# A hybrid decoder layer on one core: the first supertile of x by tokens only, turned on TensorE and scaled from PSUM; order of the adaLN staging tiles and the planner's DMA rate

## The chip, the core and the metric

One core of a Trainium2 chip runs the whole program. The engines are TensorE (PE; its weight loads are shown apart as PEld), VectorE (DVE), ScalarE (ACT), GpSimd (POOL) and SyncE (SP), which issues nearly all DMAs. The metric is the device time of one execution in microseconds (us).

## What is computed

One decoder layer on x of 4096 tokens by 1024 channels, float32. Cut to what matters here:

```python
shift, scale, gate = jnp.split(silu(c) @ ada_w + ada_b, 3, axis=-1)          # adaLN
h    = _rmsnorm(x, g_pre) * (1.0 + scale) + shift
proj = h @ w_in
attn = _sliding_window_attention(aq, ak, av, sinks) * silu(ag)
rwkv = _rwkv7_mixer(h, rr, rk, rv, ...) * silu(rg)      # recurrence over the tokens
gla  = _gla_mixer(h, gq, gkk, gv, ...) * silu(gg)
y    = jnp.concatenate([attn, rwkv, gla], axis=-1) @ w_out
return x + gate * _rmsnorm(y, g_post)
```

## The kernel before

The tokens are cut into 16 supertiles of 256. A first stage (to line 1567) makes h of each supertile, runs the GLA and RWKV-7 mixers over them in order, and stores h and the mixers' output to DRAM. A second stage does attention, the gates and the output product. The change touches the start of the first stage and, by the planner, the order of all engines.

**Precision.** A float32 matrix product is made of half-precision parts. Every weight is scaled by a power of two that comes from its sum of squares (`pow2`, line 434) and split: `hi` is a ScalarE instruction with that scale, `lo` the rest, by VectorE (`split_w`, line 731). h is split likewise into `hT[:, 0]` and `hT[:, 1]`; its power, `hscale`, comes from the adaLN vectors, and its inverse goes into the scale of each weight (`finish_w`, line 751). Each product is three: hi by hi, hi by lo, lo by hi.

**Start of the first stage.** SP loads the constants, the weights of GLA's values (`gv`), of its gate (`gk1`) and of the RWKV low-rank parts (`L`), the first 128 tokens of x (`xh`, for the sums of squares), x of supertile 0 by channels (`xt`, 1 MB, from the copy `xc` that the host has laid out), and then adaLN's matrix, 16 pieces of 128x1024 float32 (512 KB each). TensorE multiplies each piece as it lands (`adp`). Eight pieces lie in tiles of their own (`aw`); the other eight, like the weights, take staging tiles by turns from tiles that are used for something else later: the list `RING` (line 675) gives the turn, `half_tile` (line 679) takes the next. A tile that is taken twice makes the second load wait for the first one's readers. RA and UV have two tiles, KB one, and AT two that are cut in halves.

When the last piece is in, the sums are copied (`adrow`), turned (`adt`) and made into `sh` (shift) and `gs` (scale times norm weight); two ScalarE squares (`junk`), a TensorE sum (`hp`) and VectorE steps make `hscale` and `hinv`; `gs` and `sh` are multiplied by `hscale`.

**Stage a** (`stage_a`, line 1014) makes h of a supertile: squares of the tokens by rows (`ssx`), the inverse root on GpSimd (`rsx`), which TensorE turns and spreads over the partitions (`rb`), two VectorE products `xt * rb`, then for each of eight channel blocks a ScalarE instruction `xt*gs + sh`, and for each pair of blocks `hT` hi on ScalarE and lo on VectorE. The first half of supertile 0's tokens and its channels are loaded at the start, the second half of its tokens after adaLN's pieces.

**Stage p** (`stage_p`, line 1050) projects hT: `pv` (GLA values), `lp` (low rank; `x1` is read from it by VectorE), `zz` three times (k, r, v of RWKV) and `gqk` (GLA queries and keys). The weights k, r, v and gqk of the first supertile are loaded after adaLN and split in `stage_l` (line 831). `stage_d` and `stage_qa` make decays and keys (`rn`, `RA`, `KB`, with `ep` and `em`), `stage_k` turns KB (`kp`), `stage_q2` is the recurrence (`rp`, `up`, `sp`, `yp`, `yt`). The projections take turns in two PSUM tiles (`pj`).

**The planner.** Every instruction of a stage is recorded (`note`, line 99) with a modelled duration, and `pin` (line 222) plays a list schedule over all of them and fixes the order on each engine. `stage_l` has a lag of 150 places in rank (line 35). A DMA's bytes go through one modelled pipe (line 278). An engine then runs its instructions strictly in that order. As one helper emits all of them, they have the line 336 in the profile.

Of the kernel before, what the change touches and what calls it, by code (L numbers as in the profile page):

```python
# [12 lines left out]
F32 = mybir.dt.float32  # L13
# [50 lines left out]
class Order:  # L64
# [157 lines left out]
    def pin(self):  # L222

        steps = self.steps
        ready = {e: {} for e in ENGINES}
        bursts, head = {}, list(range(len(steps)))
        for k, st in enumerate(steps):
            if st.eng == "PE":
                h = head[k - 1] if k else 0
                if k and steps[h].eng == "PE" and st.joint and st.joint == steps[h].joint and st.array[0] == steps[h].array[0]:  # L230
                    head[k] = h
                bursts.setdefault(head[k], []).append(k)
        left, when = [0] * len(steps), [0.0] * len(steps)
        for k, st in enumerate(steps):
            for j in [*st.needs, *st.turn]:
                if head[j] != head[k]:
                    left[head[k]] += 1
                    steps[j].then.append(k)
        for k, st in enumerate(steps):
            if head[k] == k and not left[k]:  # L240
                ready[st.eng][k] = 0.0
        free = dict.fromkeys(ENGINES, 0.0)
        cells, mode, table, pipe, half = [0.0] * 16, None, None, 0.0, {}
        last, count = {}, 0
        while count < len(steps):
            e = min((e for e in ENGINES if ready[e]), key=lambda e: max(free[e], min(ready[e].values())))
            now = max(free[e], min(ready[e].values())) + 1e-9
            at = sorted((k for k, t in ready[e].items() if t <= now), key=lambda k: (steps[k].rank, k))
            k = at[0]
            if e == "PE" and mode is not None and steps[k].array[0] != mode:  # L250

                same = [q for q in at if steps[q].array[0] == mode]
                wait = max(now - ready[e][q] for q in at if steps[q].array[0] != mode)
                if same and (mode != (4, 4) or wait < TILING_WAIT):
                    k = same[0]
            first = max(free[e], ready[e].pop(k))
            for k in bursts.get(k, [k]):
                st, t = steps[k], max(first, free[e])
                if e == "PE":
                    m, at, passes, took, issue = st.array  # L260
                    if mode is not None and m != mode:
                        t = max(t, max(cells)) + 0.094
                    mode = m
                    t = max(t, max(cells[c] for c in at))
                    for c in at:
                        cells[c] = t + passes * took
                    free[e], st.end = t + issue * passes, t + passes * took + 0.165
                else:
                    if st.half is not None:
                        was, half[e] = half.get(e, st.half), st.half  # L270
                        if was[0] != st.half[0] or None not in (was[1], st.half[1]) and was[1] != st.half[1]:
                            t = max(t, free[e] + 0.115)
                    if st.table is not None and st.table != table:
                        t, table = max(t, free[e] + 1.28), st.table
                    free[e], st.end = t + st.occ, t + st.lat
                    if st.bytes:

                        pipe = max(pipe, t + 1.7) + st.bytes / 310e3
                        st.end = max(st.end, pipe)
                st.start = t  # L280
                if e in last:
                    self.tc.add_manual_dep(
                        st.ins, last[e], mybir.DependencyInfo(mybir.DependencyClass.NoSync, mybir.DependencyReason.DATA))
                last[e], count = st.ins.name, count + 1
                for q in st.then:
                    to, h = steps[q], head[q]
                    left[h] -= 1
                    at = t if k in to.turn else 0.0
                    if k in to.needs and e != to.eng:
                        at = max(at, st.end + HOP_FROM[e] + HOP_INTO.get(to.eng, 0.0))  # L290
                    elif k in to.needs and (e == "SP" or e != "PE" and to.needs[k]):
                        at = max(at, st.end + (0.05 if e == "SP" else 0.03))
                    when[h] = max(when[h], at)
                    if not left[h]:
                        ready[to.eng][h] = when[h]
        self.forget()
# [104 lines left out]
def hybrid_kernel(ctx, tc, x, xc, rows, ada1, adaw, w1, wl, w2, wo, cst, abias, out):  # L401
# [21 lines left out]
    def vcol(name, j=None):  # L423
        a, b = VC[name]
        return vt[:, a:b] if j is None else vt[:, a + j : a + j + 1]
# [73 lines left out]
    def t_x(name="xt"):  # L499
        return sp_.tile([P, 2, D], F32, tag="xt", name=name, bufs=1)  # L500
# [139 lines left out]
    with ExitStack() as p1:  # L640
# [14 lines left out]
        def wt(shape, name, bufs=1, dt=F32, tag=None):  # L655
            tag = tag or name
            return wk1[tag].tile(shape, dt, tag=tag, name=name, bufs=bufs)
# [14 lines left out]
            return wt(shape, name, 2, dt, "c3")  # L672


        RING = ("RA", "UV", "KB", "RA", "AT", "AT", "AT", "AT")
        stc = itertools.count()
        atq = []

        def half_tile(tag=None):
            tag = tag or RING[next(stc) % len(RING)]  # L680
            if tag == "AT":
                if not atq:
                    t = t_A([P, 2, 1024], "stg")
                    atq.extend(t[:, a, :] for a in range(2))
                t = atq.pop(0)
            else:
                t = wt([P, 1024], "stg" + tag, 2 if tag in ("RA", "UV") else 1, tag=tag)
            return t
# [14 lines left out]
        def load_tokens(i, a):  # L703
            xh = wt([P, D], "xh", 1)
            SP.dma_start(xh, x[i * NT + a * P : i * NT + (a + 1) * P, :])
            E[i]["xh"] = xh

        def load_channels(i):
            xt = E[i]["xt"] = t_x().rearrange("p a d -> p (a d)").rearrange("p (k t) -> p k t", k=KD)
            SP.dma_start(xt, xc[i])  # L710
# [11 lines left out]
        def w_pieces(n):  # L722

            r = []
            for h in range(2):
                t = half_tile()
                SP.dma_start(t, w1[:, n * 2048 + h * 1024 : n * 2048 + (h + 1) * 1024])
                r.append((slice(4 * h, 4 * h + 4), t.rearrange("p (k c) -> p k c", k=4)))
            return r
# [36 lines left out]
        mu_c = pp.tile([P, 6], F32, name="mu_c")  # L766
        V.tensor_scalar(mu_c, vcol("mu"), -1.0, 1.0, op0=ALU.mult, op1=ALU.add)

        gvp = w_pieces(0)
        gks = wt([P, KD, 16], "gk1s", 1, tag="gl")  # L770
        SP.dma_start(gks, w1src(5))
        wlt = half_tile().rearrange("p (k c) -> p k c", k=KD)
        SP.dma_start(wlt, wl)
        load_tokens(0, 0)
        load_channels(0)

        def early():
            yield from split_w("gv", gvp)
# [29 lines left out]
        def columns(j):  # L808
            return adt[:, :, j : j + 2, 0].rearrange("p c j -> p j c")

        V.tensor_tensor(sh.rearrange("p (j c) -> p j c", j=2), columns(0), vcol("bsh").rearrange("p (j c) -> p j c", j=2), op=ALU.add)
        V.tensor_tensor(gs.rearrange("p (j c) -> p j c", j=2), columns(2), vcol("bsc").rearrange("p (j c) -> p j c", j=2), op=ALU.add)
        V.scalar_tensor_tensor(gs, gs, 1.0, vcol("npre"), op0=ALU.add, op1=ALU.mult)
        hs = st.tile([P, 4], F32, tag="hs", name="hs")
        junk8 = st.tile([P, KD], F32, tag="junk8", name="junk8")
        S.activation(junk8, gs, AF.Square, scale=math.sqrt(2048.0), accum_out=hs[:, 0:1])
        S.activation(junk8, sh, AF.Square, scale=math.sqrt(2.0), accum_out=hs[:, 1:2])
        V.tensor_add(hs[:, 2:3], hs[:, 0:1], hs[:, 1:2])
        hp = mt("hp")
        PE.matmul(hp[:, 0:1], ones, hs[:, 2:3], start=True, stop=True)  # L820
        V.tensor_copy(hs[:, 3:4], hp[:, 0:1])
        pow2(hscale, hinv, hs[:, 3:4])
        V.tensor_scalar(gs, gs, hscale, None, op0=ALU.mult)
        V.tensor_scalar(sh, sh, hscale, None, op0=ALU.mult)

        for name in ("gv", "gk1", "L"):
            finish_w(name)
# [186 lines left out]
        def stage_a(i):  # L1014

            yield [("a", i - 1), ("p", i - 2)]
            e = E[i]
            ssx = st.tile([P, 2], F32, tag="ssx", name="ssx")
            for a in range(2):
                if i or a:  # L1020
                    load_tokens(i, a)
                yield [e["xh"]]
                S.activation(e["xh"], e["xh"], AF.Square, accum_out=ssx[:, a : a + 1])
            if i:
                load_channels(i)
            xt = e["xt"]
            yield [ssx]
            msx = st.tile([P, 2], F32, tag="msx", name="msx")
# [1206 lines left out]
```

## Time and profile before

| | us |
|---|---|
| three runs | 2020.94, 2021.44, 2027.34 |
| median | 2021.44 |
| the profiled execution | 2023.94 |
| its span | 2022.1 |
| granted TensorE clock over the span | 0.989 |

The profile shows one execution. Its page gives busy time by engine; the windows give the same for any stretch; the timeline lists instructions in order with start and duration, and for an idle time before an instruction what ended it. In names like `zz<-hT,rh`, the left is written and the right is read.

### The profile page before, as it was taken

The numbers are of one execution on the slowest core, as the hardware profiler recorded it, in microseconds if no ns is written. First come the engines' busy times: TensorE is split into PE (matmuls) and PEld (weight loads), VectorE is DVE, ScalarE is ACT, GpSimd is POOL, SyncE is SP. The second block draws the span as 40 slices with busy tenths as digits, with TensorE's granted clock in tenths as the row PEclk, the third lists the DMA queues.
The fourth block names the chain that finished last, engine by engine and source line by source line (L and its number), as shares of the span: only waits on it lengthen the run. The fifth ranks groups of instructions, "written<-read, shape, count | busy, mean of one in ns | idle before, by whom it ended". The sixth has DMA issues, their size and how long they took to land.

```text
span 2022.1 us, 59931 instructions
## 1 busy us (share of the span) xinstructions
PE 1919.5 (95%) x24899; PEld 1483.7 (73%) x24899; DVE 1506.7 (75%) x4246; ACT 1130.1 (56%) x2609; POOL 311.3 (15%) x485
## 2 busy tenths in 40 slices
PE   5899999999999999999989999999999999999997
PEld 1677787777787777877767678877778777787683
DVE  5777877887778887776758876777767777676866
ACT  5878778765866765555434544444454444444443
POOL 0622213262221222221100000000000000000001
PEclk8899999999999999999999999999999999999998
DMA  9464535353424411124243433344333443334414
GB/s 373 150 208 148 164 114 160 118 150 110 131 76 147 151 37 60 61 76 141 93 152 125 154 106 117 117 139 139 97 108 116 149 129 112 110 108 141 128 36 168
DMA packets 154267, 258.77 MB, mean 128 GB/s; under 512 B 49026, under 2 KB 100738, under 8 KB 147716
## 3 DMA queue, kind: packets, MB, share of 16 engines
q1 hardware_dynamic: 153844, 254.34, 38.8%
q8 instruction: 198, 3.24, 0.6%
q14 instruction: 81, 0.66, 0.1%
q10 hardware_dynamic: 144, 0.52, 0.1%
HBM read 193.98 MB, written 60.82 MB: 126 GB/s over the span
## 4 chain that ended last, share of the span: by engine, by line
PE 54%; DVE 22%; ACT 9%; DMA 8%; issue 4%; SPq 2%; POOL 1%; DVEq 0%; ACTq 0%; POOLq 0%
PE gp L336 16%; PE op L336 12%; PE zz L336 4%; PE qp L336 3%; PE pv L336 2%; PE lp L336 2%; PE kp L336 2%; PE sc L336 2%; DVE pr L336 2%; PE ovp L336 2%; DVE q L336 2%; DVE mtp L336 2%; SPq L336 2%; DMA cs<-in_wo 1%; DVE tsc L336 1%
## 5 line engine op out<-in xcount | busy, mean ns | idle before, releaser
L336 PEld LDWEIGHTS <-mtp 128*128 128x128 f16 x1344 | 130.7, 98 | 146.0 <-issue 6.3
L336 PE MATMUL op<-o,mtp 128*128 128x512 f16 x768 | 172.9, 380 | 0.0
L336 ACT ACTIVATE pr<-pr,nm,lsc 128x256 f32<-128x256 f32 (+1 forms) x256 | 149.0, 584 | 11.5 <-DVE nm L336 11.4
L336 PE MATMUL op<-ov,mtp 128*128 128x512 f16 x576 | 144.0, 381 | 3.6 <-DMA ov<-woscr 3.5
L336 PEld LDWEIGHTS <-hT 128*128 128x128 f16 x1536 | 120.5, 100 | 24.5 <-issue 3.9
L336 ACT ACTIVATE mtp<-yv,oi 128x1024 f16<-128x1024 f32 x30 | 34.5, 1149 | 155.1 <-DVE yv L336 114.4
L336 DVE CUSTOM_DVE_ANT_0 pr<-sc,ab,kept 128x256 f32<-128x256 f32 (+1 forms) x256 | 108.4, 475 | 15.5 <-PE sc L336 15.2
L336 POOL TENSOR_TENSOR ry<-sy,expo 128x1 f32<-128x1 f32 x30 | 19.1, 638 | 588.3 <-DVE sy L336 588.3
L336 PE MATMUL pv<-gvh,hT 128*128 128x272 f16 x512 | 101.0, 290 | 5.6 <-ACT hT L336 2.6
L336 DVE TENSOR_TENSOR yv<-op,yv 128x512 f32<-128x512 f32 x105 | 70.3, 681 | 47.3 <-PE op L336 33.4
L336 DVE SCALAR_TENSOR_TENSOR ag<-ag,gp 128x512 f32<-128x512 f32 x64 | 43.4, 678 | 67.8 <-ACT ag L336 67.7
L336 PE MATMUL zz<-hT,rh 128*128 128x256 f16 x512 | 91.8, 277 | 1.7 <-DVE x L336 1.7
L336 PE MATMUL lp<-hT,Lh 128*128 128x256 f16 x512 | 91.3, 274 | 1.7 <-issue 1.6
L336 PE MATMUL zz<-hT,kh 128*128 128x256 f16 x512 | 91.9, 273 | 0.0
L336 ACT ACTIVATE ag<-gp,gh 128x512 f32<-128x512 f32 x64 | 43.9, 686 | 83.3 <-PE gp L336 83.3
L336 PE MATMUL qp<-hT,q1h 128*128 128x256 f16 x512 | 86.3, 273 | 3.7 <-DVE kT L336 3.7
L336 PE MATMUL zz<-hT,vh 128*128 128x256 f16 x512 | 89.4, 275 | 0.0
L336 PE MATMUL gqk<-hT,gqkh 128*128 128x256 f16 x512 | 87.5, 273 | 1.1 <-DVE zb L336 1.1
L336 PE MATMUL gp<-hT,q5h 128*128 128x256 f16 x512 | 86.3, 273 | 0.0
L336 PE MATMUL qp<-hT,q0h 128*128 128x256 f16 x512 | 85.4, 273 | 0.0
L336 PE MATMUL gp<-hT,q3h 128*128 128x256 f16 x512 | 85.3, 273 | 0.0
L336 PE MATMUL gp<-hT,q6h 128*128 128x256 f16 x512 | 85.2, 273 | 0.0
(442 smaller groups left out, 5858.5 us busy)
## 6 DMA issues: line engine op xcount, KB each, us to landing
ov<-woscr SPq DMA_DIRECT2D x96, 512.0 KB, 4.5
xh<-in_x SPq DMA_DIRECT2D x32, 512.0 KB, 4.2
xt<-in_xc SPq DMA_DIRECT2D x16, 1024.0 KB, 8.3
hscr<-hT SPq DMA_DIRECT2D x16, 1024.0 KB, 5.0
hT<-hscr SPq DMA_DIRECT2D x16, 1024.0 KB, 4.8
x<-in_x SPq DMA_DIRECT2D x30, 512.0 KB, 4.3
out<-yv SPq DMA_DIRECT2D x30, 512.0 KB, 3.0
cs<-in_w SPq DMA_DIRECT2D x56, 256.0 KB, 3.5
```

The costliest lines, as they stand in the source:

```text
L336: r = f(*args, **kw)
```

## The change

x of supertile 0 is no longer loaded by channels. Both halves of its tokens (two loads of 512 KB into the tile of `xt`) are loaded first of all after the constants. ScalarE squares them, GpSimd makes the inverse root, VectorE scales the rows, and sixteen TensorE transposes put them by channels into four PSUM tiles, all ahead of adaLN. After adaLN, ScalarE scales from PSUM with `gs0` and `sh0`, which are not yet multiplied by `hscale`, into float32 (`hf`, in the same tile as the tokens); `hT` hi is made from that with `hscale` as its scale, and lo on VectorE with `hscale` as its column. `hscale` is thus needed one step later. `RING` now lists all turns of the start, with the AT halves ahead of RA. In `pin` a load's bytes pass at 400 instead of 310 GB/s; the same figure in the class that guides the recording (line 379) stays.

```diff
-                        pipe = max(pipe, t + 1.7) + st.bytes / 310e3
+                        pipe = max(pipe, t + 1.7) + st.bytes / 400e3
...
-        RING = ("RA", "UV", "KB", "RA", "AT", "AT", "AT", "AT")
+        RING = ("RA", "UV", "KB", *["AT"] * 4, "RA", "RA", "UV", "KB", *["AT"] * 4, "RA", "RA", "UV", "KB")
...
+        x0 = t_x()
+        for a in range(2):
+            SP.dma_start(x0[:, a], x[a * P : (a + 1) * P, :])
         gvp = w_pieces(0)
...
-        load_tokens(0, 0)
-        load_channels(0)
+
+        def first_x():
+
+            junk = wt([P, D], "xh", 1)
+            ssx = st.tile([P, 2], F32, tag="ssx", name="ssx")
+            for a in range(2):
+                S.activation(junk, x0[:, a], AF.Square, accum_out=ssx[:, a : a + 1])
+            msx = st.tile([P, 2], F32, tag="msx", name="msx")
+            V.tensor_scalar(msx, ssx, 1.0 / D, 1e-6, op0=ALU.mult, op1=ALU.add)
+            rsx = st.tile([P, 2], F32, tag="rsx", name="rsx")
+            rsqrt(rsx, msx, 2)
+            turned = []
+            for a in range(2):
+                V.tensor_scalar(x0[:, a], x0[:, a], rsx[:, a : a + 1], None, op0=ALU.mult)
+            for n, tag in enumerate(("tr", "y", "sq", "pj")):
+                tp = pst(tag, "tp").rearrange("p (a n) -> p a n", a=2)
+                for kk in range(2):
+                    k = 2 * n + kk
+                    for a in range(2):
+                        PE.transpose(tp[:, kk, a * P : (a + 1) * P], x0[:, a, k * P : (k + 1) * P], ident)
+                turned.append(tp)
+            return turned
+
+        turned = first_x()
...
+        gs0, sh0 = [cp.tile([P, KD], F32, name=n) for n in ("gs0", "sh0")]
...
-        V.tensor_scalar(gs, gs, hscale, None, op0=ALU.mult)
-        V.tensor_scalar(sh, sh, hscale, None, op0=ALU.mult)
+        V.tensor_scalar(gs, gs0, hscale, None, op0=ALU.mult)
+        V.tensor_scalar(sh, sh0, hscale, None, op0=ALU.mult)
...
+            if i == 0:
+                hT = e["hT"] = t_hT()
+                hf = x0.rearrange("p a d -> p (a d)").rearrange("p (k t) -> p k t", k=KD)
+                for kp, tp in enumerate(turned):
+                    ks = slice(2 * kp, 2 * kp + 2)
+                    for kk in range(2):
+                        k = 2 * kp + kk
+                        S.activation(hf[:, k], tp[:, kk], AF.Identity, scale=gs0[:, k : k + 1], bias=sh0[:, k : k + 1])
+                    S.activation(hT[:, 0, ks], hf[:, ks], AF.Identity, scale=hscale)
+                    V.scalar_tensor_tensor(hT[:, 1, ks], hf[:, ks], hscale, hT[:, 0, ks], op0=ALU.mult, op1=ALU.subtract)
+                    yield
+                SP.dma_start(hscr[i], hT.rearrange("p a k t -> p (a k t)"))
+                return
```

How the planned order moves, at three places. First ScalarE from the end of adaLN to the first hT; `kh` are squares of the k weights, `xh` squares of x. Before:

```order
L336 COPY adrow<-adp 128x512
L336 ACTIVATE junk_448,hs<-gs 128x8
L336 ACTIVATE junk_448,hs<-sh 128x8
L336 ACTIVATE xh,ssx<-xh 128x1024
L336 ACTIVATE kh,wss_537<-stgRA 128x1024
L336 ACTIVATE kh,wss_537<-stg 128x1024
L336 ACTIVATE xt<-xt,sh,gs 128x256 x3
L336 ACTIVATE hT<-xt 128x512
```

And of the change:

```order
L336 COPY adrow<-adp 128x512
L336 ACTIVATE junk_479,hs<-gs_473 128x8
L336 ACTIVATE junk_479,hs<-sh_474 128x8
L336 ACTIVATE xt<-tp,sh_474,gs_473 128x256 x5
L336 ACTIVATE hT<-xt,hscale 128x512 x2
L336 ACTIVATE xt<-tp,sh_474,gs_473 128x256 x2
L336 ACTIVATE hT<-xt,hscale 128x512
L336 ACTIVATE xt<-tp,sh_474,gs_473 128x256
```

The squares of x and k no longer stand between adaLN and the scaling of x. Second, VectorE where the low half of the gqk weights (`gqkl`) is made in the first supertile; `x` is `x1`, `k` and `zb` are keys and mixed projections. Before:

```order
L336 TENSOR_TENSOR xt<-xt,rb 128x1024
L336 SCALAR_TENSOR_TENSOR x_801<-lp,ivL,bl 128x256
L336 SCALAR_TENSOR_TENSOR gqkl<-stgUV,wsc,gqkh 128x1024
L336 SCALAR_TENSOR_TENSOR gqkl<-stgKB,wsc,gqkh 128x1024
L336 SCALAR_TENSOR_TENSOR gl<-gp,ga 128x256
```

And of the change, some forty rows behind `x`:

```order
L336 TENSOR_TENSOR k_1051<-k_1051,zb_800 128x512
L336 SCALAR_TENSOR_TENSOR ta<-ta,rn 128x512
L336 SCALAR_TENSOR_TENSOR sq_1143<-zb_862,first,k_1051 128x256
L336 SCALAR_TENSOR_TENSOR sq_1143<-zb_862,first,k_1051 64x256
L336 SCALAR_TENSOR_TENSOR gqkl<-stgUV,wsc,gqkh 128x1024
L336 TENSOR_TENSOR hT<-xt,hT 128x512
L336 SCALAR_TENSOR_TENSOR gqkl<-stgKB,wsc,gqkh 128x1024
```

The split of gqk has moved from beside x1 to behind the keys (`rn`, `RA`). Third, TensorE around the recurrence's first product `yp`. Before, behind the last of the gqk projection:

```order
L336 LDWEIGHTS gqkl
L336 MATMUL gqk<-hT,gqkl 128x256
L336 MATMUL yp<-Sst_502,RA 64x64 x4
L336 MATMUL kp<-first,KB 128x128 x4
L336 LDWEIGHTS hT
L336 MATMUL pv<-gvh,hT 128x272
```

And of the change, behind the last of v's projection:

```order
L336 LDWEIGHTS vl
L336 MATMUL zz<-hT,vl 128x256
L336 MATMUL yp<-Sst_533,RA 64x64 x4
L336 LDWEIGHTS gqkh
L336 MATMUL gqk<-hT,gqkh 128x256
```

The gqk projection has moved from ahead of `yp` to behind it. In the second stage the orders are the same but for a few rows.

More of the change, by code (lines that the diff above doesn't have):

```diff
@@ L679, in half_tile @@
         def half_tile(tag=None):
-            tag = tag or RING[next(stc) % len(RING)]
+            tag = tag or RING[next(stc)]
             if tag == "AT":
@@ L809, in columns @@
             return adt[:, :, j : j + 2, 0].rearrange("p c j -> p j c")
-        V.tensor_tensor(sh.rearrange("p (j c) -> p j c", j=2), columns(0), vcol("bsh").rearrange("p (j c) -> p j c", j=2), op=ALU.add)
-        V.tensor_tensor(gs.rearrange("p (j c) -> p j c", j=2), columns(2), vcol("bsc").rearrange("p (j c) -> p j c", j=2), op=ALU.add)
-        V.scalar_tensor_tensor(gs, gs, 1.0, vcol("npre"), op0=ALU.add, op1=ALU.mult)
+        gs0, sh0 = [cp.tile([P, KD], F32, name=n) for n in ("gs0", "sh0")]
+        V.tensor_tensor(sh0.rearrange("p (j c) -> p j c", j=2), columns(0), vcol("bsh").rearrange("p (j c) -> p j c", j=2), op=ALU.add)
+        V.tensor_tensor(gs0.rearrange("p (j c) -> p j c", j=2), columns(2), vcol("bsc").rearrange("p (j c) -> p j c", j=2), op=ALU.add)
+        V.scalar_tensor_tensor(gs0, gs0, 1.0, vcol("npre"), op0=ALU.add, op1=ALU.mult)
         hs = st.tile([P, 4], F32, tag="hs", name="hs")
         junk8 = st.tile([P, KD], F32, tag="junk8", name="junk8")
-        S.activation(junk8, gs, AF.Square, scale=math.sqrt(2048.0), accum_out=hs[:, 0:1])
-        S.activation(junk8, sh, AF.Square, scale=math.sqrt(2.0), accum_out=hs[:, 1:2])
+        S.activation(junk8, gs0, AF.Square, scale=math.sqrt(2048.0), accum_out=hs[:, 0:1])
+        S.activation(junk8, sh0, AF.Square, scale=math.sqrt(2.0), accum_out=hs[:, 1:2])
         V.tensor_add(hs[:, 2:3], hs[:, 0:1], hs[:, 1:2])
@@ L1017, in stage_a @@
             e = E[i]
+            if i == 0:
[11 more added lines that the diff above has]
+                return
             ssx = st.tile([P, 2], F32, tag="ssx", name="ssx")
             for a in range(2):
-                if i or a:
-                    load_tokens(i, a)
+                load_tokens(i, a)
                 yield [e["xh"]]
                 S.activation(e["xh"], e["xh"], AF.Square, accum_out=ssx[:, a : a + 1])
-            if i:
-                load_channels(i)
+            load_channels(i)
             xt = e["xt"]
```

## The prediction

> **What bounds the kernel now.** I read the page first, then the windows of stretches, then the timeline of the first 100 us on the engines that end waits there, and the waits of TensorE. The page, and one line of its chain of waits:
>
> ```profile
> span 2022.1 us, 59931 instructions
> PE 1919.5 (95%) x24899; PEld 1483.7 (73%) x24899; DVE 1506.7 (75%) x4246; ACT 1130.1 (56%) x2609; POOL 311.3 (15%) x485
> ...
> PE 54%; DVE 22%; ACT 9%; DMA 8%; issue 4%; SPq 2%; POOL 1%; DVEq 0%; ACTq 0%; POOLq 0%
> ```
>
> TensorE is the engine that sets the time. The same by stretches (span, then busy us and count by engine, granted clock, DMA share, GB/s):
>
> ```profile
> 0.00:34.50 34.50, 18.01 (x70) 3.58 (x70) 13.54 (x67) 11.97 (x20) 2.06 (x16) 1.00 0.96 372
> 34.50:43.60 9.10, 2.52 (x11) 1.71 (x11) 7.77 (x36) 6.57 (x16) 1.04 (x2) 0.65 1.03 410
> 43.60:103.00 59.40, 49.96 (x418) 38.98 (x418) 44.19 (x103) 52.13 (x100) 34.43 (x42) 0.85 0.54 173
> 103.00:1000.00 897.00, 861.67 (x14037) 694.61 (x14036) 704.53 (x2189) 606.95 (x1325) 238.09 (x372) 0.99 0.38 119
> 1000.00:2022.00 1022.00, 987.35 (x10366) 744.85 (x10366) 736.71 (x1855) 452.43 (x1152) 35.73 (x53) 0.99 0.38 122
> ```
>
> To 34.5 us DMA is the limit (0.96), to 43.6 a chain of small steps, to 103 ScalarE and VectorE feed the first supertile and TensorE is short of work by 9.4 us. From 103 it has work nearly always. So what the change wins must be won before 103 us, and be still there at 103.
>
> The steps it touches, from the timeline (start, duration, engine, line, instruction, idle before and its releaser):
>
> ```profile
> 23.19 0.33 SPq L336 DMA_DIRECT2D stgKB<-in_ada  x1
> ...
> 32.12 1.05 PE L336 MATMUL adp<-stgUV,scolb 128*32 128x512 f32 x4 [0.23 <-DMA stgUV<-in_ada]
> 33.40 1.05 PE L336 MATMUL adp<-stgKB,scolb 128*32 128x512 f32 x4 [0.23 <-DMA stgKB<-in_ada]
> 34.50 0.59 ACT L336 COPY adrow<-adp 128x512 f32<-128x512 f32 x1 [12.46 <-PE adp L336]
> 35.14 0.66 PE L336 MATMUL adt<-first,adrow 128*128 128x128 f32 x4 [0.69 <-ACT adrow L336]
> ...
> 36.95 0.18 ACT L336 ACTIVATION_READ_ACCUMULATOR junk<-sh 128x1 f32 x1
> 37.05 1.04 ACT L336 ACTIVATE xh<-xh 128x1024 f32<-128x1024 f32 x1
> ...
> 39.02 0.14 DVE L336 TENSOR_SCALAR hscale<-p2f 128x1 int32<-128x1 int32 x1
> ...
> 39.46 0.69 PE L336 MATMUL rb<-first,rsx 128*128 128x128 f32 x2 [1.49 <-POOL rsx L336]
> ...
> 41.44 1.58 ACT L336 ACTIVATE xt<-xt,sh,gs 128x256 f32<-128x256 f32 x3 [1.04 <-DVE xt L336]
> 42.93 0.61 ACT L336 ACTIVATE hT<-xt 128x512 f16<-128x512 f32 x1
> 43.60 0.41 PE L336 MATMUL pv<-gvh,hT 128*128 128x272 f16 x1 [2.55 <-ACT hT L336]
> ```
>
> **The loads.** Ahead of the last adaLN piece stood half of x by tokens (512 KB) and x by channels (1 MB); now 1 MB of tokens stands there. One 512 KB piece less, and pieces land 1.28 us apart (32.12 to 33.40): the last lands 1.28 us earlier. The other token half came after it, at no cost to it. Pieces lie in flight for 10.2 us (issue 23.19, use 33.40), about eight of them, so an issue that waits costs nothing until it is that late. In the new ring (AT tiles ahead of RA) the sixth adaLN piece that takes a ring tile waits until the first half of gv is split, with six pieces queued ahead of it and the rest of adaLN behind; the eight in flight are its cover, 10 us, beyond which each us late is a us late at the end.
>
> **Earlier work for x.** Two squares of 1.04 us (one from 37.05) move to the start; two VectorE scalings of 128x1024, with no row of this kind, cost between half and the whole of kl's 1.28 us (below) each; one power on GpSimd; sixteen transposes cost a quarter of adt's 0.66 each, 2.6 us in all. All lie in the stretch to 34.5 us, in which ScalarE was busy for 12.0 us, VectorE for 13.5 and TensorE for 18.0. The weights gv, gk1 and L come two pieces, 2.6 us, later, and are split in the same stretch; their users are pv and lp. If that cover were gone, 2.6 us would be paid.
>
> **adaLN to the first projection.** All of it is 1.28 us earlier: the junk squares end at 35.8 instead of 37.05. Then ScalarE went on to the square of x's second half, two squares of k, and an idle 1.04 us waiting for the multiplication by rb; now it scales from PSUM at once. One such instruction lies between half of hT's 0.61 (512 columns) and the SBUF form (1.58 for three, 0.53); I take 0.45, the time of zs below, a read from PSUM of this size. Five end at 38.0; hscale is there at 37.9; the first hT is done at 38.65, and pv starts at 38.7: **4.9 us earlier**, 4.5 or 5.6 by the two ends. The scaled hT is some 0.1 us longer (gqkh's 1.15 below against xh's 1.04), four times, which takes back what the reads from PSUM gain.
>
> **From there to 103 us.** The marks of before:
>
> ```profile
> 47.98 0.61 ACT L336 ACTIVATE hT<-xt 128x512 f16<-128x512 f32 x1
> 48.11 1.28 DVE L336 SCALAR_TENSOR_TENSOR kl<-stgRA,wsc,kh 128x1024 f16<-128x1024 f32 x1 [0.84 <-ACT kh L336]
> ...
> 52.29 0.38 PE L336 MATMUL lp<-hT,Lh 128*128 128x256 f16 x2
> ...
> 67.57 1.15 ACT L336 ACTIVATE gqkh<-stgUV,wsc 128x1024 f16<-128x1024 f32 x1
> ...
> 69.62 0.48 DVE L336 SCALAR_TENSOR_TENSOR x<-lp,ivL,bl 128x256 f32<-128x256 f32 x1
> 70.15 0.58 PE L336 MATMUL zz<-hT,rh 128*128 128x256 f16 x2 [1.71 <-DVE x L336]
> ...
> 71.39 1.47 DVE L336 SCALAR_TENSOR_TENSOR gqkl<-stgKB,wsc,gqkh 128x1024 f16<-128x1024 f32 x1
> 73.25 0.45 ACT L336 ACTIVATE zs<-zz,mu_s 128x256 f32<-128x256 f32 x1
> 74.37 0.42 PE L336 MATMUL zz<-hT,rl 128*128 128x256 f16 x1
> ...
> 86.09 0.38 PE L336 MATMUL gqk<-hT,gqkh 128*128 128x256 f16 x2
> ...
> 87.32 0.71 ACT L336 ACTIVATE rn<-rn,lnb 128x512 f32<-128x512 f32 x1
> 88.07 1.29 DVE L336 SCALAR_TENSOR_TENSOR rn<-zb,kkh,rn 128x256 f32<-128x256 f32 x1 [1.75 <-ACT rn L336]
> 89.88 0.47 DVE L336 SCALAR_TENSOR_TENSOR rn<-zb,kkh,rn 128x256 f32<-128x256 f32 x1
> 91.22 0.27 PE L336 MATMUL gqk<-hT,gqkl 128*128 128x256 f16 x1
> ...
> 96.22 0.39 PE L336 MATMUL pv<-gvh,hT 128*128 128x272 f16 x1 [1.40 <-DVE zb L336]
> ...
> 103.04 1.10 PE L336 MATMUL atp<-RA,KB 64*64 64x128 f32 x32
> ```
>
> ScalarE is the feeder, so I walk through its new order with these durations. The last hT is ready at 43.0 (was 48.6). TensorE needs some 7.5 us for pv, half of it at half clock, and starts lp at 46.4 (was 52.3). k's power waits behind pv on TensorE: wsc at 47.7, k split to 49.9, r's squares to 52.2, x's square and small ones to 54.5, r's wsc at 55.1, r split to 57.3, v's squares to 59.6, zs to 60.3. VectorE ends rl at 58.8, then the two multiplications of supertile 1 by 61.1, zb by 61.9, v's power, zlT, an hT half and mu by 64.5, then x1. So the r projection, which waits for x1, starts at 64.9 (was 70.15): 5.2 us ahead. From x1 to rn's second table took 17.7 us (69.62 to 87.32); the new row of work is 1 to 2 us shorter, because gqk's split (two of 1.05) has left it, its squares having come in (two of 1.1) but no wait for zs: it starts at about 81.0, **6.3 us ahead**.
>
> That lead is partly lost at gqk. Its split has moved behind this chain: rn itself (0.7), ep, em and k (six, 2.0 us by xt's 0.5 and less), two xt (1.0), then gqkh at 85.8 and, with an hT between, 87.3. VectorE has gqkl at 87.1 and 89.0. TensorE, from 64.9 on, has some 15 us of work (r's and v's projections and small products), is done with yp at 84, when RA is there, and waits for gqkl. It then runs cold: from 70.15 to 74.37 twenty instructions took 4.2 us, 0.21 each, against 0.109 in the warm gqk (47 from 86.09 to 91.22). From 87.1: 20 cold to 91.3, 28 warm to 94.4, two kp 0.95, thirty pv at 0.116 (272 columns for 256) 3.5: 98.8. Before, gqk ran early and warm, and the same thirty pv, mostly cold, ended at 103.04. **So 4.2 us are left.** One rn took 1.29 us where the next took 0.47; if that, and the like in em, falls in front of gqkl, 1 us goes. I take 3.6 with bounds 2.7 and 5.0.
>
> The cold runs by the page's windows (columns as above):
>
> ```profile
> 92.00:96.00 4.00, 0.86 (x12) 0.56 (x9) 4.00 (x8) 2.76 (x7) 3.26 (x2) 0.90 0.00 0
> 96.00:102.00 6.00, 5.78 (x26) 4.14 (x26) 5.48 (x9) 4.02 (x9) 3.90 (x5) 0.50 0.76 242
> 664.00:668.00 4.00, 1.92 (x18) 1.52 (x15) 4.00 (x23) 1.23 (x2) 2.12 (x1) 1.00 0.59 197
> 668.00:672.00 4.00, 2.94 (x16) 2.02 (x20) 3.20 (x7) 1.78 (x4) 3.06 (x6) 0.58 0.51 149
> ```
>
> After 3.1 us of idle in 92 to 96 the clock is granted at 0.50; the change's idle ahead of gqk is longer, so gqk starts at half clock. The Trainium skill (TensorE: Matmul & The Clock Gate, "Part 1: The HAM clock gate") speaks against the change in this: an idle window of about 3.4 us puts the array at half rate, and about 3.4 us of work brings it back. By its 3.4 us instead of the trace's 4.2 the cold run would cost 1.7 and not 2.1 us, and the gain would be 0.4 us more; the trace agrees on the half rate.
>
> **Behind 103 us.** No instruction is added; the planned order of the first stage is written anew for all engines, by the shifted start and the faster modelled transfers. How its waits fall cannot be read. What one is worth can: in 664 to 672 TensorE is idle for 3.1 us and then loses 0.42 of 2.9 us to the clock, 1.2: 4.4 us. Such places more or fewer are the main unknown. The second stage stands nearly as before.
>
> **The sum.** Against the profiled execution (2023.9 us, its span and 1.8 around it) -3.6 gives 2020.3. The median of the runs is 2021.4, 2.5 us lower, and gives **2017.8 us**. The bound of 0.3%, about what a measurement of this kernel can tell from no change, is 6.1 us: below 2015.4 or above 2027.5.
>
> **Rivals.** (1) Forecast: -3.6 at 103 us, as many long waits later as before: 0.45. (2) One long wait of the first stage goes, because the chain of supertile 1 keeps more lead than TensorE: -3.6 - 4.4 = -8.0, 2013.4. For it speaks that ScalarE and VectorE come to 98 us with more lead than TensorE; against it that most later waits lie on the recurrence, which the start does not touch: 0.27. (3) The lead is lost altogether at gqk: if rn's second table is not early, gqkh ends at 93.4 and gqkl at 94.7, TensorE runs from 93.1 cold, and thirty pv end at 104.8: +1.8, 2023.2. The adaLN stream not shortened, as by a queue that refills with a gap, would be a part of this; the steady 1.28 us speak against it: 0.10. (4) Slower: the new order puts TensorE in front of the recurrence or of KB too early, with an idle stretch and a cold run of 4.4 us each time as at 664. The first costs more than the gain: +0.8, 2022.2; with two it is 2026.6, with three 2031. That 35 us are idle in the 897 us before, in many small waits, speaks for a new order that is about as good: one 0.10, more 0.08.
>
> **Numbers.** The range of 2011.0 to 2026.0 holds (1) with its bounds, (3), one place of (4) and all of (2) but its lower edge; some 0.18 is left out. Faster by over 0.3%: (2) and a small part of (1), 0.33. Slower by over 0.3%: the upper half of (4), 0.08. Within: 0.59.
>
> **What would show it.** Right: last adaLN product at 32.1; pv's first at 38.7; lp at 46.4; r's projection at 64.9, released by x1; TensorE waiting for gqkl near 87, cold; atp's stretch 4 us ahead. Wrong: gqk not waited for, and 6 us ahead at 100; or the lead at 100 there, but other idle time between 103 and 1000 than 35.3 us by more than 4.

## The result, and the profile after

The change is slower: a median of 2035.4 us (6 runs, 2033.3 to 2036.3) against 2022.2 for the kernel before beside it (6 runs). The ratio of the runs is 1.0056, with a 95% interval of 1.0045 to 1.0068, that is 9 to 14 us, some 11 (the medians lie 13 apart). The prediction gave slower by over 0.3% a chance of 0.08. The profiled execution took 2033.3 us, 9.4 more than that of before. In the page:

```profile
span 2031.6 us, 59968 instructions
PE 1923.3 (95%) x24913; PEld 1486.3 (73%) x24913; DVE 1511.5 (74%) x4246; ACT 1131.6 (56%) x2609; POOL 306.4 (15%) x485
...
PE 55%; DVE 21%; DMA 9%; ACT 8%; issue 4%; SPq 2%; POOL 1%; DVEq 0%; ACTq 0%; POOLq 0%
```

The shares hardly move; where the time went cannot be seen there. The windows of the stretches that the prediction showed, after the change (columns as there):

```profile
0.00:34.50 34.50, 20.62 (x90) 6.92 (x90) 16.86 (x76) 13.93 (x22) 3.10 (x18) 1.00 0.96 377
34.50:43.60 9.10, 5.46 (x33) 3.77 (x34) 6.00 (x23) 8.77 (x21) 0.00 (x0) 0.81 1.03 416
43.60:103.00 59.40, 47.04 (x448) 37.61 (x449) 45.70 (x108) 49.50 (x94) 33.02 (x43) 0.86 0.53 178
103.00:1000.00 897.00, 854.58 (x13851) 685.34 (x13843) 695.55 (x2136) 600.53 (x1310) 230.96 (x369) 0.99 0.38 118
```

Up to 103 us TensorE has done more than before (571 instructions by the three rows against 499, 16 of them the new transposes). From 103 to 1000 us it does less: busy 854.6 us where it was 861.7, 13,851 instructions where there were 14,037. The start, in the timeline of TensorE (start, duration, instruction, idle before and its releaser):

```profile
31.70 1.05 PE L336 MATMUL adp<-stgKB,scolb 128*32 128x512 f32 x4 [0.23 <-DMA stgKB<-in_ada]
33.44 0.66 PE L336 MATMUL adt<-first,adrow 128*128 128x128 f32 x4 [0.69 <-ACT adrow L336]
38.38 0.41 PE L336 MATMUL pv<-gvh,hT 128*128 128x272 f16 x1 [2.31 <-ACT hT L336]
...
45.78 0.38 PE L336 MATMUL lp<-hT,Lh 128*128 128x256 f16 x2
...
64.04 0.61 PE L336 MATMUL zz<-hT,rh 128*128 128x256 f16 x2
...
83.92 0.69 PE L336 MATMUL yp<-Sst,RA 64*64 64x64 f32 x8 [3.67 <-DVE RA L336]
85.50 0.61 PE L336 MATMUL gqk<-hT,gqkh 128*128 128x256 f16 x2 [0.89 <-ACT gqkh L336]
88.65 0.39 PE L336 MATMUL gqk<-hT,gqkl 128*128 128x256 f16 x1 [2.54 <-DVE gqkl L336]
...
99.29 1.10 PE L336 MATMUL atp<-RA,KB 64*64 64x128 f32 x32
```

This is the start that was forecast: the last adaLN piece 1.7 us earlier, `pv` 5.2, `lp` 6.5, the r projection 6.1, then the wait for `gqkl`, and `atp` at 99.29 instead of 103.04, 3.75 us ahead where 3.6 was taken. At the first KB (the second factor of the recurrence, made by VectorE) the lead, by which the change is ahead of the kernel before at the same instruction, is 2.4 us (91.0 instead of 93.4). The last product of the first stage (`yt` of supertile 15) then comes at 1049.5 us instead of 1038.4, 11 us late; the second stage adds nothing. So in these two executions the start wins some 3 us, and 14 are lost between 100 us and the end of the first stage, on the same instructions. From the `atp` stretch to that `yt` TensorE takes 950.2 us instead of 935.4: it idles for 45.4 us instead of 36.9, and the same work keeps it busy for 904.8 instead of 898.4. Part of the second is the clock, which is at half for 17.1 us there instead of 10.2. In one stretch TensorE gets 8.5 us less done, first of before, then of after:

```profile
400.00:640.00 240.00, 232.10 (x3779) 187.49 (x3775) 197.53 (x591) 167.89 (x370) 80.50 (x121) 0.99 0.39 120
```

```profile
400.00:640.00 240.00, 223.63 (x3568) 179.12 (x3566) 190.80 (x566) 158.50 (x353) 77.01 (x114) 0.98 0.35 107
```

It idles 16.4 us there instead of 7.9. The longest of these waits can be followed through three engines. TensorE and what it waits for, after the change:

```profile
496.63 0.27 PE L336 MATMUL gqk<-hT,gqkl 128*128 128x256 f16 x1
499.99 1.09 PE L336 MATMUL yt<-first,ysb 128*128 128x128 f32 x4 [3.09 <-DVE ysb L336]
500.87 0.63 PE L336 MATMUL gqk<-hT,gqkh 128*128 128x256 f16 x2
```

VectorE, which makes `ysb`:

```profile
493.77 0.17 DVE L336 BATCH_NORM_AGGREGATE mv<-bst 128x2 f32<-128x6 f32 x1
496.47 0.49 DVE L336 SCALAR_TENSOR_TENSOR zb<-zz,mu_c,zs 128x256 f32<-128x256 f32 x1 [2.53 <-ACT zs L336]
496.87 0.16 DVE L336 TENSOR_SCALAR ve<-mv 128x8 f32<-128x8 f32 x1
496.94 0.69 DVE L336 TENSOR_TENSOR ysb<-ysb,mv 128x512 f32<-128x512 f32 x1
```

And ScalarE, which makes `zs`:

```profile
491.00 0.74 ACT L336 ACTIVATE ch<-cs,wsc 128x512 f16<-128x512 f32 x1
494.99 0.72 ACT L336 ACTIVATE ch<-cs,wsc 128x512 f16<-128x512 f32 x1 [3.24 <-DMA cs<-in_w]
495.61 0.82 ACT L336 ACTIVATE zs<-zz,mu_s 128x256 f32<-128x256 f32 x2
```

ScalarE stands at the split of a weight piece (`cs`, for the second stage, wanted by nobody soon) that has not landed. SP had issued it at 488.76 us, 6.2 us before the split could start. `zs` stands behind it, `zb` waits for `zs`, `ysb` stands behind `zb` on VectorE, and TensorE's `yt` stands ahead of a projection that it could have gone on with. Then it runs cold, by the window behind it:

```profile
500.00:504.00 4.00, 4.00 (x18) 2.92 (x19) 3.44 (x7) 2.24 (x4) 1.68 (x2) 0.50 0.00 0
```

The same place in the kernel before, on ScalarE:

```profile
486.79 0.74 ACT L336 ACTIVATE ch<-cs,wsc 128x512 f16<-128x512 f32 x1
487.41 0.85 ACT L336 ACTIVATE zs<-zz,mu_s 128x256 f32<-128x256 f32 x2
488.63 0.72 ACT L336 ACTIVATE ch<-cs,wsc 128x512 f16<-128x512 f32 x1 [0.37 <-DVE bst L336]
```

There `zs` stands ahead of the second piece, and `yt` (492.98) follows the projection with no wait. On ScalarE one pair of rows has changed places; on TensorE the last products of the projection now stand behind `yt`, and the second piece was issued at 485.30, 3.3 us before its split.

### The profile page after: what moved, and what is told of

Its sections match the earlier page's. It is cut to its first block, busy times and chain, and to the rows that moved or that the text cites. A ratio compares the mean times of both kernels' runs of the same rounds, so it can differ in the third digit from the quotient of the medians.

```text
span 2031.6 us, 59968 instructions
## 1 busy us (share of the span) xinstructions
PE 1923.3 (95%) x24913; PEld 1486.3 (73%) x24913; DVE 1511.5 (74%) x4246; ACT 1131.6 (56%) x2609; POOL 306.4 (15%) x485
## 4 chain that ended last, share of the span: by engine, by line
PE 55%; DVE 21%; DMA 9%; ACT 8%; issue 4%; SPq 2%; POOL 1%; DVEq 0%; ACTq 0%; POOLq 0%
PE gp L336 16%; PE op L336 12%; PE zz L336 4%; PE qp L336 3%; PE gqk L336 2%; PE kp L336 2%; PE sc L336 2%; PE pv L336 2%; DVE mtp L336 2%; PE ovp L336 2%; DVE q L336 2%; DVE tsc L336 2%; PE lp L336 2%; DMA AS<-adr 2%; SPq L336 2%
## 5 line engine op out<-in xcount | busy, mean ns | idle before, releaser
L336 DVE CUSTOM_DVE_ANT_0 pr<-sc,ab,kept 128x256 f32<-128x256 f32 (+1 forms) x256 | 108.3, 475 | 14.9 <-PE sc L336 14.6
```

Of the source, the lines that this page charges most:

```text
L336: r = f(*args, **kw)
```

## The experiments

Three theories at first. **Rate theory**: the start wins its 3 us, and the order that 400 GB/s makes the planner write for the rest of the first stage loses 14. **Start theory**: the new start itself leaves the engines badly to one another, whatever the rate. **Scatter theory**: any moved number gives another order, and orders lie some us apart by chance. Each run was timed in five rounds beside the kernel before; a ratio of 1.001 is 2.0 us, and in brackets stands the 95% interval. What a profile shows is one execution of the run. Late and early in the planner mean its own times, which differ from the trace's by some per cent.

**1 to 4: the planner's rate.** In the change (1, 3, 4) or in the kernel before (2):

```diff
-                        pipe = max(pipe, t + 1.7) + st.bytes / 400e3
+                        pipe = max(pipe, t + 1.7) + st.bytes / 310e3
+                        pipe = max(pipe, t + 1.7) + st.bytes / 355e3
+                        pipe = max(pipe, t + 1.7) + st.bytes / (400e3 if t < 100.0 else 310e3)
...
-                        pipe = max(pipe, t + 1.7) + st.bytes / 310e3
+                        pipe = max(pipe, t + 1.7) + st.bytes / 400e3
```

> The change with the planner's old rate of 310 GB/s. Rate theory: the start wins about 3 us up to 100 us in any case, and the 14 us that are lost between 200 and 700 us come from the order that the 400 GB/s figure sets; so this kernel is 3 us faster than the one before, ratio 0.9985, and its last yt is 3 us ahead. Start theory: the loss comes from the new start itself (gqk split late, another lead of the engines over one another), whatever the rate: +11 us, ratio 1.0055, as the change. Scatter theory: every change of a modelled number writes another order, and such orders lie some 5 us either side of one another with no cause in the number itself: anything from 0.997 to 1.006.

Measured: 1.0041 (1.0027 to 1.0054), +8.3 us.

> The kernel before with 400 GB/s in the planner, nothing else. Rate theory: +14 us, ratio 1.007, with the loss between 200 and 700 us. Start theory: within 2 us of before, ratio 0.999 to 1.001. Scatter theory: anything from 0.997 to 1.006, with the extra idle places at supertiles of its own and not at the change's.

Measured: 1.0072 (1.0051 to 1.0092), +14.6 us, without anything of the new start.

> The change with 355 GB/s, half way. Rate theory: between the change and the change with 310, about +4 us, ratio 1.002. Start theory: +11 us, 1.0055. Scatter theory: no relation to its two neighbours; it may be below or above both by 5 us.

Measured: 1.0058 (1.0041 to 1.0075), +11.7 us.

> The change with 400 GB/s for transfers that the planner starts in its first 100 us and 310 behind that. If the rate costs by the loads of supertiles 2 to 9 (tokens, channels, weight pieces modelled as landing too early, so that their users are put too far ahead), this gives -3 us, 0.9985, as with 310 throughout. If it costs by the start of the order, +11 us, 1.0055, as the change. Scatter theory: neither, anything from 0.997 to 1.006.

Measured: 1.0021 (1.0009 to 1.0033), +4.2 us.

The second run by itself shows that another order of the very same instructions can cost 14 us. Neither the rate theory nor the start theory names all four numbers: with 310 the change still loses, and the start cannot be why the kernel before loses. The range of the scatter theory (0.997 to 1.006) holds three of them, and the interval of the fourth reaches into it; but so wide a range is hard to miss.

**5 to 7: start and order apart.** What rate and scatter have in common is the **order theory**: the loss is in the order behind the start, whatever made it. For these runs the order of the first stage is read from a table, not played:

```diff
     def pin(self):
-
+        if PLAN: return replay(self)
```

`replay` chains each engine's instructions in the listed sequence by the same scheduling-only dependencies as `pin`. Each instruction is known by its stage, supertile and place within both, so an order of one kernel can be put on the other.

> The change's instructions and its order for what the planner starts in its first 95 us (the first supertile); behind that every engine's order in the first stage is that of the kernel before, written down as a table. Order theory (the start wins, the order that the planner rewrites behind it loses): the change leads by 2.4 us at the first KB and keeps that, so 2.4 us faster than before, ratio 0.9988, between 0.998 and 0.9995. Start theory (the loss comes from the start itself, from how it leaves the engines to one another): about +11 us as the change, 1.0055.

Measured: 0.9997 (0.9985 to 1.0008), -0.6 us. The start theory is out: the same start with the old order behind it loses nothing. It wins nothing that can be told from none, either.

> The other way round: the kernel before up to the planner's 103 us, its start and its first supertile untouched, and behind that the order of the change, as a table. Order theory: the change falls from 2.4 us ahead to 11.3 behind between 100 us and the end of the first stage, so +13.7 us, ratio 1.0068. Start theory: no difference, 0.999 to 1.001.

Measured: 1.0099 (1.0079 to 1.0119), +20 us. The old start with the new order loses all of it, and 6 us more than expected. Its windows from 103 to 200 us and from 400 to 640:

```profile
103.00:200.00 97.00, 89.99 (x1309) 70.93 (x1307) 66.14 (x219) 70.34 (x160) 21.70 (x37) 0.96 0.57 181
...
400.00:640.00 240.00, 224.05 (x3564) 179.97 (x3565) 192.24 (x572) 160.92 (x357) 78.31 (x117) 0.99 0.34 104
```

In 400 to 640 it is busy for 224.1 us, as the change (223.6). The extra falls at the seam, in 103 to 200 (clock 0.96). That an order written for an earlier start waits when the start is late would explain it; no run tests this by itself.

> The change with its own order up to about 420 us of the trace (the planner's 385), and the order of the kernel before behind that. Order theory, and the loss where the traces show it (7 us in 430 to 510, 4 in 560 to 630): +2.6 us remain, ratio 1.0013. If the loss is not bound to the places of that order but follows from the lead that the engines have over one another at 420 us, it is lost in the old order too: +11 us, 1.0055.

Measured: 1.0031 (1.0018 to 1.0043), +6.3 us, which is neither number. The profiled execution (2036.4 us, 5.6 above the run's median) had a lead of only 0.8 us at the first KB (92.65 instead of 93.44), and it is 4 behind at 440 us and 5.3 at 600. So the 7 us of 430 to 510 and the 4 of 560 to 630 are not there when the old order takes over: in this execution that loss is bound to the order at those places. From 880 us on it loses another 4, in the old order.

The run with the new start and old order shows what such a place costs in any order. Its lead is 2.7 us at the first KB and 6.1 at the KB of supertile 13; then this, at supertile 14:

```profile
875.60 1.12 PE L336 MATMUL op<-Gst,qg 128*64 128x256 f32 x4 [3.21 <-DVE qb L336]
```

```profile
872.00:876.00 4.00, 0.79 (x16) 0.55 (x14) 1.13 (x6) 0.00 (x0) 0.13 (x1) 0.80 0.13 37
876.00:880.00 4.00, 4.00 (x58) 3.00 (x55) 3.15 (x17) 0.37 (x1) 0.00 (x0) 0.50 0.00 0
```

After 3.2 us of idle the clock is granted at 0.50, and the lead falls to 2.1 us: one place, 4 us.

**8 to 12: is it the rate, or chance?** A rate of 312 says nothing new of the chip, but writes the order anew.

```diff
-                        pipe = max(pipe, t + 1.7) + st.bytes / 310e3
+                        pipe = max(pipe, t + 1.7) + st.bytes / 312e3
```

> The kernel before with the planner's rate at 312 instead of 310 GB/s, 0.6 per cent, which says nothing new of the chip, but writes the first stage's order anew. Scatter theory (orders written by the same planner lie apart by chance, and the one of the kernel before lies at the good end): slower than before by 3 to 14 us like the other rewritten orders, about 1.004. Rate theory (the 400 GB/s figure misplaces what waits for loads): within 1 us of before, 0.9995 to 1.0005.

Measured: 0.9984 (0.9969 to 0.9999), -3.2 us. The scatter theory as it was put here was wrong: it is not slower, and the order of the kernel before is not at the good end. By its middle it is outside the 1 us of the rate theory too, but its interval ends just inside, so 3 us of scatter are not shown by this run alone.

> The change's instructions, its order for what the planner starts in its first 95 us, and behind that the order that the kernel before gets with 312 GB/s in the planner (3.3 us faster than before in the run of that order). Order theory, if a start's lead and an order's gain add up: 2.7 us of lead at the first KB and 3.3 us of the order, some of the lead spent at a wait as in the run with the order of before (there 0.6 us were left of 2.7): 3 to 6 us faster than before, ratio 0.9970 to 0.9985, and faster than either kernel. If start and order cannot be joined freely (an order is only good for the start it was written for, as the run with the old start and the new order lost 6 us more than the change itself): no faster than before, 1.000 to 1.004.

Measured: 0.9987 (0.9976 to 0.9997), -2.6 us: with the run above, the fastest of all, and faster than both kernels. But start and order did not add up; at the first KB it had no lead at all (93.50 us), which the last section comes back to.

> The kernel before with 395 GB/s in the planner, beside the run with 400 (+14.5 us). Rate theory, in its weaker form (a rate near 400 is bad because what waits for loads is then put too far ahead): +12 to +15 us, ratio 1.006 to 1.0075. Scatter theory (the number matters only as a seed): no relation to the neighbour, anything from -4 to +15 us; under +8 us would speak for it.

Measured: 1.0070 (1.0055 to 1.0085), +14.2 us, as the rate theory had it.

> The change with 402 instead of 400 GB/s in the planner; some 2,600 of TensorE's 28,165 rows stand otherwise. Rate theory: as the change, +10 to +13 us against before. Scatter theory: between -3 and +15 us; a difference of over 4 us from the change would speak for it.

Measured: 1.0071 (1.0057 to 1.0085), +14.4 us, near the change (+11.3) and by its middle 1.4 us above the rate theory's range.

> The change with 312 GB/s in the planner, beside the run of the change with 310 (+8.3 us). Rate theory: +7 to +9 us. Scatter theory: between -3 and +15 us; a difference of over 4 us from the run with 310 would speak for it, as the kernel before shows one of 3.3 us between 310 and 312.

Measured: 0.9996 (0.9986 to 1.0007), -0.8 us, 9 us from the same kernel with 310. This is scatter, and more than the intervals allow for.

So chance can be worth 9 us from one seed (a moved number) to the next, and yet the rate counts: five kernels with 355 to 402 behind the start lost 11.3 to 14.6 us, five with 310 or 312 there lay between -3.2 and +8.3 (the kernel before itself among them).

**13 to 16: how early the planner takes loads to land.** A further theory, the **wait theory** (the scatter theory is called seed theory beside it): with a high rate the planner puts ScalarE's work on loaded pieces ahead of where they land, as in the rows of 491 us, and everything behind it comes late. What the loads take in the kernel before, from its DMA issues (KB each, median us from issue to landing):

```profile
xh<-in_x SPq DMA_DIRECT2D x26, 512.0 KB, 3.9
xt<-in_xc SPq DMA_DIRECT2D x13, 1024.0 KB, 8.3
cs<-in_w SPq DMA_DIRECT2D x47, 256.0 KB, 3.4
```

The planner has at least 3.5, 4.8 and 2.6 for these, at either rate, and more only where its pipe is full.

```diff
+                        pipe = max(pipe, t + 1.7) + st.bytes / (400e3 if t < 100.0 else 250e3)
+                        pipe = max(pipe, t + 1.7) + st.bytes / (400e3 if t < 100.0 else 200e3)
+                        pipe = max(pipe, t + 1.7) + st.bytes / (310e3 if t < 100.0 else 250e3)
...
+            ... st.lat = {("xt", 1024): 8.0, ("xh", 512): 4.0, ("cs", 256): 3.6, ("cs", 128): 2.7}.get((... , kb), st.lat) if len(self.steps) > 900 else st.lat
```

> The change with 400 GB/s for the planner's first 100 us and 250 behind that. Wait theory (ScalarE stands in order before loads that have not landed; the more cautious the modelled rate, the less): ScalarE's waits for DMA between 103 and 1030 us fall from 53.8 us to below 45, and the time to within 4 us of before, 0.998 to 1.002. Seed theory: unrelated to the rate, anywhere between 0.998 and 1.007, and as likely above 1.004 as below it.

Measured: 0.9999 (0.9984 to 1.0013); ScalarE's waits for DMA, summed over the rows of the waits, 30.0 us (53.8 in the change, 42.5 in the kernel before).

> As the run before it with 200 GB/s behind 100 us. Wait theory: ScalarE's waits for DMA below 40 us, time 0.997 to 1.002. Seed theory: anywhere between 0.998 and 1.007.

Measured: 1.0030 (1.0017 to 1.0043), waits 14.7 us: the fewest waits, and 6.1 us slower than before.

> The kernel before with 310 GB/s in the planner's first 100 us and 250 behind that. Wait theory: ScalarE's waits for DMA at or below the 42.5 us of before, time 0.997 to 1.002. Seed theory: anywhere between 0.998 and 1.007.

Measured: 1.0004 (0.9992 to 1.0015), waits 32.8 us.

> The change with its 400 GB/s, but behind the first supertile the planner's landing times for the loads of x by channels, x by tokens and the weight pieces are 8.0, 4.0 and 3.6 (128 KB: 2.7) us, near the medians of the trace (7.8 to 8.3, 3.9 to 4.0, 3.4 to 3.7), instead of 4.8, 3.5 and 2.6 (2.3). Wait theory: ScalarE's waits for DMA below 42 us in spite of the 400, and 7 to 13 us of the loss gone, ratio 0.998 to 1.003. Seed theory: anywhere between 0.998 and 1.007. Rate theory by another way (stores and their buffers, the recurrence's small transfers): +8 us or more, above 1.004, whatever ScalarE waits.

Measured: 1.0013 (1.0000 to 1.0025), waits 40.5 us. With the loads' measured landing times, 400 GB/s costs 2.6 us and not 11. That is 8.7 us less, but the step from 310 to 312 moved the change by 9, so this one run cannot be told from a lucky order.

Three of four as the wait theory had it, and against it the run with 200. All four also lie in the range of the seed theory, so they do not part the two.

**17 and 18: the waits taken away, the order kept.** The pieces get a third tile and SP issues their loads earlier; the other four engines have the order of the change (17) or of before (18), row for row, by the table.

```diff
-            s32 = wt([P, 512], "cs", 2)
+            s32 = wt([P, 512], "cs", 3)
...
-            left, right = [wt([P, 512], "cs", 2).rearrange("p (h n) -> p h n", h=2) for _ in range(2)]
+            left, right = [wt([P, 512], "cs", 3).rearrange("p (h n) -> p h n", h=2) for _ in range(2)]
```

> The change with its own order on TensorE, VectorE, ScalarE and GpSimd, row for row; the weight pieces for the second stage (cs) have three tiles instead of two, and SP issues their loads 3.1 us earlier on the average, at most 4.5. Wait theory: ScalarE's waits for these pieces fall from 47.4 us to below 20, and with them 6 to 12 of the 11 to 13 us go: ratio 0.9995 to 1.003. Rival (the loss lies in how TensorE, VectorE and ScalarE are ordered against one another, and the waits for loads only go along with it): the waits fall, the time does not: 1.0045 or more.

Measured: 1.0043 (1.0026 to 1.0060), +8.7 us, next to the rival's 1.0045 and above the wait theory's range. ScalarE's waits for DMA (us in total, times, longest) in the change, from 103 to 1030 us:

```profile
ACT ch L336 <- DMA cs<-in_w: 34.0, 19, 4.2
ACT ch L336 <- DMA cs<-in_wo: 13.4, 11, 2.8
ACT xh L336 <- DMA xh<-in_x: 3.8, 8, 1.0
ACT ch L336 <- DMA woscr<-ch: 2.6, 3, 1.4
```

And with the loads earlier:

```profile
ACT ch L336 <- DMA wscr<-ch: 8.0, 5, 2.9
ACT xh L336 <- DMA xh<-in_x: 7.1, 7, 2.6
ACT ch L336 <- DMA woscr<-ch: 5.7, 5, 1.9
ACT ch L336 <- DMA cs<-in_w: 5.7, 3, 4.1
ACT ch L336 <- DMA cs<-in_wo: 1.5, 2, 1.3
```

> The same on the kernel before: its own order on the four engines, three tiles for the pieces, loads 3.3 us earlier on the average. Its ScalarE waits 24.3 us for these pieces, half of the change's; below 10 is expected. Wait theory: 1 to 5 us faster, ratio 0.9975 to 0.9995. Rival: no difference, 0.9995 to 1.0005.

Measured: 1.0026 (1.0011 to 1.0041), +5.3 us, with 4.0 us of these waits left of 24.3; neither side had it slower.

In the change too the waits for the pieces are nearly gone (7.2 us left of 47.4; those for `ch` tiles whose store has not landed, `wscr<-ch`, are new), and the place at 497 us has shrunk to 1.0 us of idle. The time has not followed: 2.6 us less than the change by the ratios, within their intervals of none. The edit has a cost of its own, since on the kernel before it loses 5.3 us, with SP's queue as the only one that is ordered otherwise. If it costs the change as much, the waits were worth up to 8 of the 11 us; if it costs the change nothing, 2.6. So that ScalarE's waits for loads are the whole of it is not shown, and the run with 200 speaks against it. Over all kernels the waits go along with the loss only in the large: the six with 53 us of them or more lost 11 us or more, the others, with 15 to 51, lay between -3 and +9 in no order.

**What stays open.** That the loss is in the order behind 100 us is shown (runs 5 and 6; run 2 shows that an order alone can cost as much). That a high modelled rate gives worse orders is shown as a tendency, by five kernels against five. That the measured landing times cure most of it is not shown: the one run that has it so is within the scatter. By which of the many changed places the rate does it is not settled.

## Why the prediction was wrong

**The loads, the start, gqk: right.** In the profiled execution: last adaLN product at 31.7 (32.1 forecast), `pv` at 38.4 (38.7), `lp` at 45.8 (46.4), r's projection at 64.0 (64.9), `yp` at 83.9 (84), the cold wait for `gqkl` at 88.65 (87.1 to 89.0), `atp` 3.75 us ahead (3.6). That one execution comes so close is partly luck. Ten of the profiled executions have the change's order on TensorE, VectorE and ScalarE up to 100 us (the change, runs 4, 5, 7, 9, 11, 13, 14, 16 and 17): their first KB lies between 90.2 and 93.7 us, 91.9 on the average. The four with the order of before (the kernel before, runs 6, 15 and 18) have it at 93.4 to 95.0, 94.1 on the average. So the start wins 2.3 us there, and 3.5 at `atp` (100.6 instead of 104.1), as forecast, but a single execution can as well show nothing of it. Ring, squares, scalings and transposes were hidden, as said. One was right by a wrong path: r's projection was not released by `x1`, which VectorE starts at 65.27, after it; it ran in front of `x1`, behind `zp`, which waited 2.96 us for a weight's `wtot` and started at 61.93.

**"Behind 103 us. ... How its waits fall cannot be read": the step that failed.** That it could not be read was true; what was made of it was not. The argument was that 35 us of idle in many small waits "speaks for a new order that is about as good". The runs give the scale that was missing: orders by the same planner, ten of them over the instructions of the one kernel or the other with rates between 310 and 402, lie from 3 us faster than before to 15 slower, and those with a rate of 355 or more all at the slow end. Against that spread, a gain of 3.6 us at the start decides nothing, and the order was not a remainder with a chance of 0.18 but the largest term: 14 us here, put at nothing in the sum.

**Rival (4) had the place and the sign, not the size.** Its mechanism, TensorE put in front of something that is not ready, idle and then cold, is what the profile shows at 497 us (3.1 us of idle, then half clock to 504). Its price of 4.4 us a place was about right (875 us in the run with the old order: 4 us). Its count was not: it stopped at three places, with a chance of 0.08 for two or more. From 103 to 1000 us TensorE idles 42.4 us instead of 35.3, and 14 of its idle times, 25 us in all, are of 1 us or more, where before had 8 with 14. And the edit of one number, 310 to 400, was given no term, although it is part of the change and makes the planner trust in loads that it should not: the trace of before has 1 MB of x by channels landing in a median of 8.3 us and the 256 KB pieces in 3.4, against the planner's 4.8 and 2.6. That could have been read, though not what it would cost: the same times stand in the planner at 310 GB/s.

**The sign that was to tell.** "The lead at 100 there, but other idle time between 103 and 1000 than 35.3 us by more than 4": it is 7.1 more.

## What to carry to other kernels

Where a planner fixes the order of every engine, an edit that shifts its input is two changes: what the edit does, and a new draw of the order. Before weighing a gain of a few us, measure the draw: time the same kernel with a number of the planner moved by half a per cent, and put the old order on the new kernel by a table; here the old order turned 11 us slower into no difference (0.6 us faster, within the interval). And check a planner's landing times against those from issue to landing in the trace before raising a rate: 400 GB/s cost 11 us, and 2.6 with the measured times beside it, though that may be one lucky order.

## What the runs showed of the hardware

How long TensorE stays cold after an idle stretch varies with where its work starts. Runs 5 and 9 have the same order up to 100 us. In run 5 `pv` starts at 38.42 us:

```profile
38.42 0.41 PE L336 MATMUL pv<-gvh,hT 128*128 128x272 f16 x1 [2.31 <-ACT hT L336]
```

The windows in which its clock falls and rises:

```profile
38.00:39.00 1.00, 0.58 (x2) 0.13 (x2) 0.67 (x2) 1.00 (x3) 0.00 (x0) 0.57 1.03 410
41.00:42.00 1.00, 1.00 (x8) 0.78 (x7) 0.27 (x1) 1.00 (x3) 0.00 (x0) 0.73 1.02 418
```

In run 9 at 39.10:

```profile
39.10 0.41 PE L336 MATMUL pv<-gvh,hT 128*128 128x272 f16 x1 [2.31 <-ACT hT L336]
```

```profile
37.00:38.00 1.00, 0.00 (x0) 0.00 (x0) 0.84 (x7) 1.00 (x4) 0.00 (x0) 0.86 1.05 422
44.00:45.00 1.00, 1.00 (x8) 0.75 (x7) 0.06 (x1) 1.00 (x3) 0.00 (x0) 0.73 1.05 375
```

Between these rows the clock is at 0.50. The clock records of the traces hold 0.50 and 1.00 alone, so run 5 was at half from 38.1 to 41.5 us, 3.4 us, and run 9 from 37.7 to 44.5, 6.8 us: once and twice the same length. The records of the twenty traces say so throughout. Apart from the one that ends each trace, they have 159 stretches at half clock: 93 of 3.4 us, 39 of 6.8, 26 of 10.2 and one of 13.7. So the clock changes in steps of 3.4 us. In run 5 `pv` starts 0.3 us after such a step, in run 9 1.4 us after it, and there the array stays cold for a whole step more. Run 5 worked cold for 3.1 us, run 9 for 5.4; `lp` came 1.8 us later (45.81 and 47.62), 0.7 by the start and some 1.1 by the half clock, and the first KB 2.8 us later (90.70 and 93.50).

The Trainium skill (TensorE: Matmul & The Clock Gate, "What's actually happening") says that the gate looks at windows of 3.4 us that run freely and do not start with the work, so that the moment of the switch depends on where in one the first product falls. The traces agree with the window, but its figure of 500 ns either way is too small here: the two cold runs differ by 2.3 us. The prediction's cold stretch of 4.2 us, from 70.15 to 74.37, lies in one of 6.8, from 67.9 to 74.7. A lead of 2 or 3 us at 100 us, read in one execution, is no more certain than such a step.
